# Down phase of a feed-forward layer: weight loads, block sums and residual tiles tied to other steps

## The chip, the cores and the metric

The program runs on one core of one Trainium2 chip, and nothing else runs beside it. The metric is the device time of one execution in microseconds. Lower is better. The time given for a kernel is the median of several executions; a profiled execution is one further execution, with its own time.

## What is computed

The kernel is one layer of a hybrid encoder on 2048 tokens of width 1024, in fp32: a mixing part (an FFT convolution and a bidirectional mLSTM), a cross-attention, and a feed-forward part with residual and a final normalization. Only the last part matters here:

```
h = h + square(relu(rms_norm(h, norm_ff_g) @ ff_w1)) @ ff_w2      # ff_w1: 1024 x 4096, ff_w2: 4096 x 1024
return rms_norm(h, final_norm_g)
```

## The kernel before

**Products in threes.** A matmul in full fp32 is made of three faster ones. A tile is split in a rounded high part and the remainder (`halves`, line 1620): ScalarE casts (L1622) and VectorE or GpSimd subtracts (L1623). `mm3` (line 352) then multiplies `ah` with `bh` (L354), `ah` with `bl` (L357) and `al` with `bh` (L358), in this order, where `ah` and `al` are the parts of a weight tile, `bh` and `bl` those of an activation tile. Both rings are short: four pairs of `ah`/`al`, six of `bh`/`bl`; the raw tiles `wr` that they are split from have six buffers (`raw`, line 1615).

**The feed-forward part** (`ffn`) works by a scheme of seven block products in place of eight. In the up phase the hidden activations and their combinations are written to DRAM (`hc`). The down phase multiplies them by combinations of the four quarters of each block of `ff_w2`. It goes over four blocks `o` of the hidden dimension. Each has seven products `i` in the order 1, 6, 7, 5, 3, 2, 4, each product has two token halves `tp`, and each of these four steps `k`. So there are 4 x 7 x 2 x 4 = 224 steps `s`, 56 for a block, eight for a product. A step is 12 matmuls on TensorE. Its result is gathered in four PSUM banks (named `mm` for the first token half and `hy` for the second) and, after the fourth step, added into the tile `acc[i, tp]` (line 1944).

**What a step writes beside its matmuls** (the loop over `down`, from line 1918):

- `fetch_b(s + 3)`: loads the activation tile of the step three further on (`wr<-hc`, L1617) and splits it (`bh`, `bl`).
- In the second token half `fetch_a(n + 1, k)`: makes the weight tile for the next product. For products 1, 6, 7 and 5 it comes from the twelve resident tiles `WD[k, 0..2]` (named `w` in the rows; a ring of 12 buffers), for 3, 2 and 4 it is loaded (`wr<-in_ff_w`, L1617), and for 3 `WD[k, 0]` is subtracted from it in place (L1750). The subtractions of `fetch_a` are VectorE's for the first six products and GpSimd's from the seventh on (product 4 of the first block).
- In product 2, first token half: `load_w(o + 1, k)` loads the three resident tiles of the next block for this `k` (L1757, SP's queue).
- In product 4, first token half: `sums_w(k)` forms two sums of them on GpSimd (L1760, L1761).
- From step 4 on, one `residual(i, tp, k)`: loads a tile of the residual stream into `acc` (`acc<-h`, L1867) and scales it on GpSimd (L1868); for i = 4 a second GpSimd operation follows (L1870). There are 32 of them, in the order i = 7, 4, 3, 2.

**What sets the order.** The code is written step by step, but a scheduler decides each engine's order by a simulated timeline, and puts an instruction as early as its inputs and buffers let it. A method `behind` (L362) holds an instruction back: it adds a dependency on the last matmul written so far, so that the scheduler places the instruction after that matmul. The dependency is of a class without synchronization: it shapes the order and leaves no semaphore wait on the chip. The loads are issued by SP, which works through its queue in order, as do the other engines.

Of the kernel before, what the change touches and what calls it, by code (L numbers as in the profile page):

```python
# [14 lines left out]
ALU = mybir.AluOpType  # L15
# [118 lines left out]
class Prog:  # L134
# [1592 lines left out]
    def ffn(self):  # L1727
        nc, tc, a = self.nc, self.tc, self.a
# [24 lines left out]
        def load_w(o, k):  # L1753
            w = self.blocks_of(2, 4 * o + k)
            for j, src in enumerate((w[0][0], w[1][0], w[1][1])):
                t = self.WD[k, j] = self.wtile()
                nc.sync.dma_start(out=t, in_=src)  # L1757

        def sums_w(k, op=nc.gpsimd.tensor_tensor):
            op(self.WD[k, 2], self.WD[k, 1], self.WD[k, 2], ALU.add)  # L1760
            op(self.WD[k, 1], self.WD[k, 0], self.WD[k, 1], ALU.subtract)  # L1761

        def fetch_b(s, eng=nc.vector):
            n, tp, k = down[s]
            o, i = prods[n]
            bq[s] = self.halves(self.raw(hc[tp, i - 1, 4 * o + k]), ("bh", "bl"), 6, eng)

        with tc.tile_pool(name="up", bufs=1) as U:
# [26 lines left out]
            for n, (tp, g, i) in enumerate(steps):  # L1795
# [11 lines left out]
                if n + 9 >= len(steps) and n + 5 < len(steps):  # L1807
                    load_w(0, n + 9 - len(steps))
                if n + 2 >= len(steps):
                    k = n + 2 - len(steps)  # L1810
# [20 lines left out]
                else:  # L1831
# [5 lines left out]
                    t = [self.stage() for _ in range(4)]  # L1837
                    op = nc.gpsimd.tensor_tensor
# [11 lines left out]
        with tc.tile_pool(name="down", bufs=1) as B:  # L1850
            acc, ms = {}, []
            on = [B.tile([128, D], F32, tag="on", name="on", bufs=2) for _ in range(2)]
            for tp in range(2):
                for h in range(2):
                    v = on[tp][:, 512 * h:512 * h + 512]
                    nc.sync.dma_start(out=v, in_=msd[2 * tp + h])
                    ms.append(v)
            for i in (1, 6, 7, 4, 5, 3, 2):
                for tp in range(2):
                    acc[i, tp] = B.tile([128, 4, 512], F32, tag="acc", name="acc", bufs=14)  # L1860
            gl = B.tile([128, D], F32, name="gl")
            nc.scalar.dma_start(out=gl, in_=a["final_norm_g"].unsqueeze(0).broadcast_to([128, D]))

            def residual(i, tp, k):
                n, h = {2: (0, 0), 7: (1, 1), 3: (1, 0), 4: (0, 1)}[i]
                v = acc[i, tp][:, k]
                nc.sync.dma_start(out=v, in_=h2[2 * tp + n, :, 4 * h + k])  # L1867
                nc.gpsimd.tensor_tensor(v, v, ms[2 * tp + n], ALU.mult)  # L1868
                if i == 4:
                    nc.gpsimd.tensor_tensor(v, v, acc[7, tp][:, k], ALU.subtract)  # L1870

            ss = B.tile([128, 4, 2, 4], F32, name="ss")

            def turn(c, h, src, dst, t, tag):
                pt = self.ps.tile([128, 512], F32, tag=tag, name=tag, bufs=4)
                for k in range(4):
                    nc.tensor.transpose(pt[:, 128 * k:128 * k + 128], src[:, k, 128 * t:128 * t + 128], self.ident)
                junk = B.tile([128, 512], F32, tag="junk", name="junk", bufs=1)
                nc.scalar.activation(junk, pt, AF.Square, accum_out=ss[:, c, h, t:t + 1])
                nc.vector.tensor_tensor(dst[:, t], pt, gl[:, 512 * h:512 * h + 512], ALU.mult)  # L1880

            def finish(c, dst):
                m = B.tile([128, 4], F32, tag="mo", name="mo", bufs=2)
                q = self.rbp[:, 4 * c:4 * c + 4]
                for h in range(2):
                    nc.vector.scalar_tensor_tensor(m, ss[:, c, h], 1.0 / D, m if h else q, ALU.mult, ALU.add)
                rv = self.rsqrt(B, m, "or")
                for t in range(4):
                    for h in range(2):
                        v = dst[h][:, t]  # L1890
                        if h and c % 2 == 0:
                            nc.vector.tensor_scalar(v, v, rv[:, t:t + 1], None, ALU.mult)
                        else:
                            nc.scalar.mul(v, v, rv[:, t:t + 1])
                        if t % 2:
                            r0 = 512 * c + 128 * (t - 1)
                            (nc.sync if h and c % 2 == 0 else nc.scalar).dma_start(
                                out=self.out[r0:r0 + 256, 512 * h:512 * h + 512].rearrange("(t p) c -> p t c", p=128),
                                in_=dst[h][:, t - 1:t + 1])

            def turned(c, tp, h, i, j, dst=None):
                def one(tag, t):
                    turn(c, h, acc[i, tp], acc[j, tp], t, tag)
                    if dst and t == 3:
                        finish(c, dst)
                return [lambda tag, t=t: one(tag, t) for t in range(4)]

            def add(i, j, tp, eng):
                for m in range(4):
                    eng.tensor_tensor(acc[i, tp][:, m], acc[i, tp][:, m], acc[j, tp][:, m], ALU.add)  # L1910

            early = [(i, tp, k) for i in (7, 4, 3, 2) for tp in range(2) for k in range(4)]
            outs = []
            V, G = nc.vector, nc.gpsimd
            for s, (n, tp, k) in enumerate(down):
                o, i = prods[n]
                if n == 0 and tp == 0:
                    sums_w(k, nc.vector.tensor_tensor)
                if s + 3 < len(down):
                    fetch_b(s + 3, G if s > 199 and k else V)  # L1920
                if o < 3 and tp == 0 and i == 2:
                    load_w(o + 1, k)
                if o < 3 and tp == 0 and i == 4:
                    sums_w(k)
                if early and s > 3:
                    residual(*early.pop(0))
                if k == 0:
                    bank = [self.hy() if tp else self.mm() for _ in range(4)]
                (ah, al), (bh, bl) = aq[n, k], bq.pop(s)
                for m in range(4):  # L1930
                    msl = slice(128 * m, 128 * m + 128)
                    self.mm3(bank[m], ah[:, msl], al[:, msl], bh, bl, k == 0, k == 3)
                if tp and n + 1 < len(prods):
                    fetch_a(n + 1, k)
                for _ in range(min(len(outs), 2 if len(outs) > 4 or n + 1 == len(prods) else 1)):
                    outs.pop(0)("mm" if tp else "hy")
                if k < 3:
                    continue
                for m in range(4):
                    v = acc[i, tp][:, m]  # L1940
                    if o == 0 and i in (1, 6, 5):
                        nc.scalar.copy(v, bank[m])
                    else:
                        d = nc.vector.tensor_tensor(v, bank[m], v, ALU.add)
                        if s + 1 == len(down):
                            tc.keep_in_program_order(d)
                if o < 3:
                    continue
                if i == 1:
                    add(2, 1, tp, G)  # L1950
                elif i == 6:
                    add(6, 1, tp, V)
                elif i == 7:
                    add(7, 6, tp, V)
                    add(3, 6, tp, G)
                elif i == 5:
                    add(3, 5, tp, V)
                    add(5, 7, tp, G)
                    add(4, 7, tp, G)
                    if tp:  # L1960
                        outs += turned(1, 0, 1, 5, 1)
                elif i == 3:
                    c = 2 * tp + 1
                    if not tp:
                        outs += turned(3, 1, 1, 5, 1)
                    outs += turned(c, tp, 0, 3, 6, (acc[6, tp], acc[1, tp]))
                elif i == 2:
                    outs += turned(2 * tp, tp, 0, 2, 7)
                elif i == 4:
                    outs += turned(2 * tp, tp, 1, 4, 5, (acc[7, tp], acc[5, tp]))  # L1970
            for x in outs:
                x("mm")
# [126 lines left out]
```

## Time and profile before

| what | value |
|---|---|
| time, median of 3 executions | 3133.62 us (3127.82 to 3135.12) |
| time of the profiled execution | 3131.11 us, its span 3129.0 us |
| mean granted clock of TensorE | 0.989 |
| busy share of the span: TensorE, its weight loads, VectorE, ScalarE, GpSimd | 97%, 76%, 63%, 48%, 37% |
| start of the down phase in the trace | about 2478 us |
| data moved | 607.07 MB, mean 194 GB/s |

How to read the rows: a row of a timeline has the start in us, the duration in us, the engine, the line, the operation, the tile written and the tiles read, and the count; in square brackets stands how long the engine stood idle before it and what ended that. Engines are PE (TensorE), PEld (its weight loads), DVE (VectorE), ACT (ScalarE), POOL (GpSimd) and SPq (SP's queue of DMA issues, with the time of issuing, not of the transfer). A row of a group has the count, then the busy time in us and the mean of one in ns, then the idle time before. A row of the windows has the stretch, its length, the busy time of PE, PEld, DVE, ACT and POOL, each with its number of instructions, then the granted clock of TensorE, the busy share of the DMA engines, and GB/s. A row of waits has who waited for whom, the us in total, how often, and the longest.

### The profile page before, as it was taken

Reading aid. Unit: us, or ns where it says so; the run is one execution under the profiler, and the core shown is the slowest. Engines: PE = TensorE matmul, PEld = TensorE weight load, DVE = VectorE, ACT = ScalarE, POOL = GpSimd, SP = SyncE. Lnnn points to the kernel's source line nnn. Section 1 sums busy time; section 2 is a strip of 40 time slices with the busy share of each in tenths; the row PEclk is TensorE's granted clock in tenths of the full one; section 3 lists DMA queues with packets and bytes.
Section 4 is the critical chain, followed back from the end, with each engine's and each line's share of the span. In section 5 each row is a group of like instructions: output and inputs, shape, how many; then the busy total and the mean of one; then the engine's idle time right before and its main releaser. Section 6 shows DMA issues by size and latency. Waiting matters only on the chain.

```text
span 3129.0 us, 42943 instructions
## 1 busy us (share of the span) xinstructions
PE 3029.1 (97%) x14257; PEld 2374.5 (76%) x14257; DVE 1964.8 (63%) x3448; ACT 1489.6 (48%) x2907; POOL 1146.9 (37%) x802
## 2 busy tenths in 40 slices
PE   8999999989999898999999999999999999999998
PEld 6655667766677666888887888888888878888876
DVE  7965466446646456777674656657545686555695
ACT  5443366533656225555544455556555533333335
POOL 0122012200113244324141337766456393434493
PEclk9999999999999999999999999999999999999999
DMA  6464767666878897455375657657644574434324
GB/s 212 153 210 163 235 203 220 194 215 216 241 206 249 261 316 245 145 190 186 127 268 186 217 166 243 207 178 231 205 152 153 179 234 142 152 123 152 122 91 172
DMA packets 444101, 607.07 MB, mean 194 GB/s; under 512 B 38494, under 2 KB 248542, under 8 KB 442856
## 3 DMA queue, kind: packets, MB, share of 16 engines
q1 hardware_dynamic: 405988, 546.54, 54.3%
q10 hardware_dynamic: 37892, 57.79, 5.3%
q8 instruction: 113, 1.85, 0.2%
q14 instruction: 108, 0.88, 0.1%
HBM read 401.79 MB, written 202.41 MB: 193 GB/s over the span
## 4 chain that ended last, share of the span: by engine, by line
PE 81%; DMA 7%; DVE 6%; ACT 3%; issue 2%; POOL 1%; SPq 0%; ACTq 0%; DVEq 0%; POOLq 0%
PE mm L354 17%; PE mm L358 17%; PE mm L357 17%; PE hy L358 5%; PE hy L354 5%; PE hy L357 5%; PE hy L177 3%; PE mm L912 1%; PE hy L943 1%; PE hy L985 1%; DMA xt<-in_x_t_dram 1%; DVE bl L1623 1%; PE mm L674 1%; DMA a<-hy 1%; PE mm L703 1%
## 5 line engine op out<-in xcount | busy, mean ns | idle before, releaser
L1623 DVE TENSOR_TENSOR bl<-wr,bh 128x512 fp32r<-128x512 f32 x213 | 239.8, 1132 | 132.5 <-ACT bh L1622 132.3
L1622 ACT CAST ah<-w 128x512 fp32r<-128x512 f32 x284 | 176.9, 624 | 302.5 <-PE hy L357 155.8
L365 DVE TENSOR_TENSOR wl<-wn,wh 128x512 fp32r<-128x512 f32 (+1 forms) x300 | 217.6, 772 | 102.7 <-ACT wh L365 102.4
L354 PE MATMUL mm<-xh,wh 128*128 128x512 f32 x640 | 267.7, 419 | 12.2 <-ACT wh L365 9.1
L990 POOL TENSOR_TENSOR b<-b,a 128x512 f32<-128x512 f32 x64 | 87.0, 1362 | 510.1 <-ACT b L988 320.0
L357 PE MATMUL mm<-xl,wh 128*128 128x512 f32 x640 | 255.8, 400 | 0.7 <-DVE xl L365 0.6
L1622 ACT CAST bh<-wr 128x512 fp32r<-128x512 f32 x232 | 143.8, 622 | 234.6 <-PE mm L358 176.2
L358 PE MATMUL mm<-xh,wl 128*128 128x512 f32 x640 | 255.0, 399 | 0.0
L1623 DVE TENSOR_TENSOR al<-w,ah 128x512 fp32r<-128x512 f32 x236 | 217.6, 922 | 54.9 <-ACT ah L1622 54.9
L358 PE MATMUL mm<-bh,al 128*128 128x512 f32 x576 | 224.1, 392 | 6.8 <-DVE al L1623 4.3
L354 PE MATMUL mm<-bh,ah 128*128 128x512 f32 x576 | 225.7, 392 | 0.5 <-DVE acc L1780 0.4
L357 PE MATMUL mm<-bl,ah 128*128 128x512 f32 x576 | 224.9, 390 | 0.0
L365 ACT CAST wh<-wn 128x512 fp32r<-128x512 f32 (+1 forms) x300 | 167.4, 620 | 110.4 <-PE mm L358 52.1
L357 PE MATMUL mm<-act,wh 128*128 128x512 f32 x512 | 200.5, 393 | 0.8 <-DVE act L365 0.8
L354 PE MATMUL mm<-act,wh 128*128 128x512 f32 x512 | 198.4, 393 | 1.1 <-ACT wh L365 0.9
L358 PE MATMUL mm<-act,wl 128*128 128x512 f32 x512 | 199.1, 392 | 0.3 <-DVE wl L365 0.3
L354 PE MATMUL hy<-bh,ah 128*128 128x512 f32 x448 | 175.2, 391 | 0.0
L357 PE MATMUL hy<-bl,ah 128*128 128x512 f32 x448 | 174.6, 390 | 0.0
L358 PE MATMUL hy<-bh,al 128*128 128x512 f32 x448 | 174.4, 390 | 0.0
L354 PEld LDWEIGHTS mm<-xh,wh 128*128 128x128 f32 x640 | 121.4, 190 | 67.6 <-issue 19.0
L354 PE MATMUL mm<-wh,xh 128*128 128x256 f32 (+1 forms) x512 | 155.7, 305 | 13.0 <-ACT xh L365 10.6
L336 POOL TENSOR_TENSOR b<-b 128x512 f32<-128x512 f32 x32 | 58.3, 1822 | 277.8 <-DVE b L333 137.2
(369 smaller groups left out, 8285.4 us busy)
## 6 DMA issues: line engine op xcount, KB each, us to landing
wr<-hc SPq DMA_DIRECT2D x224, 256.0 KB
w<-in_ff_w_dram SPq DMA_DIRECT2D x172, 256.0 KB
hc<-wn SPq DMA_DIRECT2D x128, 256.0 KB
wn<-in_w_in_dram SPq DMA_DIRECT2D x100, 256.0 KB
hc<-q SPq DMA_DIRECT2D x96, 256.0 KB
fs<-a SPq DMA_DIRECT2D x32, 512.0 KB
a<-fs SPq DMA_DIRECT2D x64, 256.0 KB
a<-zs SPq DMA_DIRECT2D x64, 256.0 KB
```

Source lines behind the costliest of these rows:

```text
L177: b = self.nc.tensor.matmul(*products[-1], start=True, stop=True)
L336: nc.gpsimd.tensor_tensor(e[1], f, b, ALU.subtract)
L354: first = mm(ps, lh, rh, start=start, stop=False)
L357: mm(ps, lh, rl, start=False, stop=False)
L358: self.last = mm(ps, ll, rh, start=False, stop=stop)
L365: both = (self.nc.scalar.copy(hi, src), self.nc.vector.tensor_tensor(lo, src, hi.bitcast(F32), ALU.subtract))
L674: mul(p[:, m], w[:, k, ms], mt[k // 4][:, k % 4], start=k == 0, stop=k == 7)
L703: mul(p, t[:, m, ms], o_[:, m, ds], start=m == 0, stop=m == 1)
L912: nc.tensor.matmul(pp, dm[:, m], t[:, m], start=True, stop=True)
L990: nc.gpsimd.tensor_tensor(xt, xt, hi[:, m], ALU.mult)
L1622: self.nc.scalar.copy(hi, src)
L1623: eng.tensor_tensor(lo, src, hi.bitcast(F32), ALU.subtract)
```

## The change

Three things are edited. The weight loads of the blocks 1 to 3 are held behind the last matmul written before them, which bars the scheduler from placing them ahead of the step in product 2 that they are written in. The eight sums of each next block on GpSimd are held the same way, in product 4. And from step 20 on a residual tile is written in two of three steps, not in each.

```
-                nc.sync.dma_start(out=t, in_=src)
-
-        def sums_w(k, op=nc.gpsimd.tensor_tensor):
-            op(self.WD[k, 2], self.WD[k, 1], self.WD[k, 2], ALU.add)
-            op(self.WD[k, 1], self.WD[k, 0], self.WD[k, 1], ALU.subtract)
+                d = nc.sync.dma_start(out=t, in_=src)
+                if o:
+                    self.behind(d)
+
+        def sums_w(k, op=nc.gpsimd.tensor_tensor, late=False):
+            a = op(self.WD[k, 2], self.WD[k, 1], self.WD[k, 2], ALU.add)
+            b = op(self.WD[k, 1], self.WD[k, 0], self.WD[k, 1], ALU.subtract)
+            if late:
+                self.behind(a)
+                self.behind(b)
...
                 if o < 3 and tp == 0 and i == 4:
-                    sums_w(k)
-                if early and s > 3:
+                    sums_w(k, late=True)
+                if early and (3 < s < 20 or s > 19 and s % 3):
                     residual(*early.pop(0))
```

Line numbers behind the edit grow by two to five: L1760, L1761, L1868 and L1944 of before are L1762, L1763, L1873 and L1949 of the change, L1867 and L1870 are L1872 and L1875. The numbers behind tile names are counted through the program and differ a little between the two.

**First place: the weight tiles of product 3 in the first block.** On SP, before: `wr_23074` and `wr_23101` are the third and fourth of the four weight tiles that product 3 loads, the `wr` from `hc` are activation tiles, `w` are resident tiles of the next block, `acc_22315` and `acc_22316` are residual tiles of i = 2.

```order
L1617 DMA wr_23074<-in_ff_w2_dram 128x512
L1617 DMA wr_23081<-hc_16691 128x512
L1757 DMA w_23388<-in_ff_w2_dram 128x512
L1867 DMA acc_22315<-h2_10617 128x512 x4
L1617 DMA wr_23101<-in_ff_w2_dram 128x512
L1617 DMA wr_23112<-hc_16691 128x512
L1757 DMA w_23390<-in_ff_w2_dram 128x512
```

The same stretch of SP in the change, from the same third weight tile (here `wr_23066`) on; the fourth is `wr_23093`.

```order
L1617 DMA wr_23066<-in_ff_w2_dram 128x512
L1617 DMA wr_23073<-hc_16691 128x512
L1617 DMA wr_23093<-in_ff_w2_dram 128x512
L1617 DMA wr_23104<-hc_16691 128x512
L1617 DMA wr_23128<-hc_16691 128x512
L1617 DMA wr_23146<-hc_16691 128x512
L1617 DMA wr_23166<-hc_16691 128x512
L1617 DMA wr_23190<-hc_16691 128x512
L1872 DMA acc_22315<-h2_10617 128x512 x3
L1617 DMA wr_23212<-in_ff_w2_dram 128x512
```

The loads of `w` have left this stretch, and the residual tiles of i = 2 stand behind five activation tiles that follow the fourth weight tile. VectorE at the same place, before (`al_23024` is the first weight tile of product 3, ready for TensorE):

```order
L1750 TENSOR_TENSOR wr_23074<-wr_23074,w_22103 128x512
L1623 TENSOR_TENSOR bl_23030<-wr_23027,bh_23029 128x512
L1623 TENSOR_TENSOR bl_23057<-wr_23054,bh_23056 128x512
L1750 TENSOR_TENSOR wr_23101<-wr_23101,w_22127 128x512
L1623 TENSOR_TENSOR al_23024<-wr_23020,ah_23023 128x512
```

and in the change:

```order
L1750 TENSOR_TENSOR wr_23066<-wr_23066,w_22103 128x512
L1623 TENSOR_TENSOR bl_23024<-wr_23021,bh_23023 128x512
L1750 TENSOR_TENSOR wr_23093<-wr_23093,w_22127 128x512
L1623 TENSOR_TENSOR bl_23051<-wr_23048,bh_23050 128x512
L1623 TENSOR_TENSOR al_23018<-wr_23014,ah_23017 128x512
```

The fourth L1750 has moved ahead of one `bl`; the first `al` still stands behind it. Nothing else moves on VectorE, and the orders of TensorE and ScalarE are the same as before.

**Second place: GpSimd in the first block.** Before, from the residual tiles of i = 3, second half, on; the sums of the next block are L1760 and L1761:

```order
L1868 TENSOR_TENSOR acc_22314<-acc_22314,on_22298 128x512 x4
L1760 TENSOR_TENSOR w_23314<-w_23312,w_23314 128x512
L1760 TENSOR_TENSOR w_23342<-w_23340,w_23342 128x512
L1761 TENSOR_TENSOR w_23312<-w_23310,w_23312 128x512
L1761 TENSOR_TENSOR w_23340<-w_23338,w_23340 128x512
L1760 TENSOR_TENSOR w_23366<-w_23364,w_23366 128x512
L1761 TENSOR_TENSOR w_23364<-w_23362,w_23364 128x512
L1868 TENSOR_TENSOR acc_22315<-acc_22315,on_22297 128x512 x4
L1760 TENSOR_TENSOR w_23390<-w_23388,w_23390 128x512
L1761 TENSOR_TENSOR w_23388<-w_23386,w_23388 128x512
L1868 TENSOR_TENSOR acc_22316<-acc_22316,on_22298 128x512 x4
L1623 TENSOR_TENSOR al_23433<-wr_23430,ah_23432 128x512
```

and in the change, from the same residual tiles on; the `al` are the four weight tiles of product 4:

```order
L1873 TENSOR_TENSOR acc_22314<-acc_22314,on_22298 128x512 x4
L1873 TENSOR_TENSOR acc_22315<-acc_22315,on_22297 128x512 x4
L1873 TENSOR_TENSOR acc_22316<-acc_22316,on_22298 128x512 x4
L1623 TENSOR_TENSOR al_23433<-wr_23430,ah_23432 128x512
L1623 TENSOR_TENSOR al_23457<-wr_23454,ah_23456 128x512
L1762 TENSOR_TENSOR w_23308<-w_23306,w_23308 128x512
L1763 TENSOR_TENSOR w_23306<-w_23304,w_23306 128x512
L1623 TENSOR_TENSOR al_23481<-wr_23478,ah_23480 128x512
L1762 TENSOR_TENSOR w_23338<-w_23336,w_23338 128x512
L1623 TENSOR_TENSOR al_23505<-wr_23502,ah_23504 128x512
L1762 TENSOR_TENSOR w_23364<-w_23362,w_23364 128x512
L1763 TENSOR_TENSOR w_23336<-w_23334,w_23336 128x512
```

The eight sums have moved from among the residual tiles to behind the second `al` of product 4; three of them stand ahead of the last two `al`. In the other two blocks the sums move to the same place.

**Third place: the loads of the next block on SP, in the second block.** Before (names without numbers here, since only the kinds matter), from the loads in product 7 on:

```order
L1757 DMA w<-in_ff_w_dram 128x512 x2
L1617 DMA wr<-hc 128x512
L1757 DMA w<-in_ff_w_dram 128x512
L1617 DMA wr<-hc 128x512 x5
L1617 DMA wr<-in_ff_w_dram 128x512
L1757 DMA w<-in_ff_w_dram 128x512
L1617 DMA wr<-hc 128x512
L1757 DMA w<-in_ff_w_dram 128x512 x3
L1617 DMA wr<-in_ff_w_dram 128x512
```

and in the change, where all twelve stand beside product 2 (the `wr` from `in_ff_w` are weight tiles of product 4):

```order
L1617 DMA wr<-hc 128x512 x3
L1757 DMA w<-in_ff_w_dram 128x512 x3
L1617 DMA wr<-hc 128x512 x2
L1757 DMA w<-in_ff_w_dram 128x512 x3
L1617 DMA wr<-in_ff_w_dram 128x512
L1617 DMA wr<-hc 128x512
L1757 DMA w<-in_ff_w_dram 128x512 x3
L1617 DMA wr<-in_ff_w_dram 128x512
L1617 DMA wr<-hc 128x512
L1757 DMA w<-in_ff_w_dram 128x512 x3
```

The loads that were strewn over some twenty `wr` loads from product 7 to product 3 now stand in four triples.

## The prediction

> **What bounds the kernel.** I read the page's busy table first, then the down phase in slices of 100 us, then TensorE's own waits there.
>
> ```profile
> span 3129.0 us, 42943 instructions
> PE 3029.1 (97%) x14257; PEld 2374.5 (76%) x14257; DVE 1964.8 (63%) x3448; ACT 1489.6 (48%) x2907; POOL 1146.9 (37%) x802
> ```
>
> ```profile
> 2400.00:2500.00 100.00, 99.51 (x437) 81.62 (x437) 61.97 (x82) 49.85 (x86) 44.08 (x30) 1.00 0.50 167
> 2500.00:2600.00 100.00, 95.75 (x416) 78.83 (x416) 79.47 (x75) 41.15 (x73) 77.25 (x48) 0.98 0.71 238
> 2600.00:2700.00 100.00, 100.00 (x443) 82.84 (x442) 57.26 (x73) 32.98 (x56) 33.55 (x25) 1.00 0.38 120
> 2900.00:3000.00 100.00, 100.00 (x443) 82.84 (x442) 69.97 (x81) 31.94 (x54) 55.82 (x37) 1.00 0.35 108
> ```
>
> ```profile
> PE mm L358 <- DVE al L1623: 4.3, 1, 4.3
> PE mm L354 <- DVE acc L1780: 0.4, 1, 0.4
> ```
>
> The change acts only between the start of the down phase, near 2478, and the loads of its last block. From 2600 to 3000 TensorE is busy in every microsecond at the full granted clock (1.00), so nothing is to be won there. The waits of TensorE from 2478 to 3000 are two, and one of them is 4.3 us long. All that the change can win is this one wait and what hangs on it. Here it is, on TensorE's own timeline:
>
> ```profile
> 2564.87 0.39 PE L354 MATMUL mm<-bh,ah 128*128 128x512 f32 x1
> 2565.10 0.39 PE L357 MATMUL mm<-bl,ah 128*128 128x512 f32 x1
> 2569.74 0.79 PE L358 MATMUL mm<-bh,al 128*128 128x512 f32 x1 [4.25 <-DVE al L1623]
> 2570.33 0.63 PE L354 MATMUL mm<-bh,ah 128*128 128x512 f32 x1
> ...
> 2572.88 0.39 PE L354 MATMUL mm<-bh,ah 128*128 128x512 f32 x1
> ```
>
> Matmuls start 0.227 us apart (2564.87 to 2565.10), so a step of 12 takes 2.72 us. The third matmul of step 32 (product i = 3, first k) was due at 2565.33 and came at 2569.74, 4.41 us late, because it needs `al` from VectorE. Behind it seven starts lie 0.43 to 0.59 us apart: at 0.227 us they would have brought TensorE from 2565.33 to 2566.92, and the trace has 2572.88. So the stall costs **5.96 us**: 4.41 of waiting and 1.55 of slow matmuls. Who made `al` late?
>
> ```profile
> 2553.92 3.47 DVE L1623 TENSOR_TENSOR bl<-wr,bh 128x512 fp32r<-128x512 f32 x2
> 2558.39 0.70 DVE L1750 TENSOR_TENSOR wr<-wr,w 128x512 f32<-128x512 f32 x1 [0.99 <-DMA wr<-in_ff_w_dram]
> 2559.01 3.47 DVE L1623 TENSOR_TENSOR bl<-wr,bh 128x512 fp32r<-128x512 f32 x2
> 2567.19 0.82 DVE L1750 TENSOR_TENSOR wr<-wr,w 128x512 f32<-128x512 f32 x1 [4.70 <-DMA wr<-in_ff_w_dram]
> 2567.93 1.75 DVE L1623 TENSOR_TENSOR al<-wr,ah 128x512 fp32r<-128x512 f32 x1
> 2575.28 0.68 DVE L1623 TENSOR_TENSOR bl<-wr,bh 128x512 fp32r<-128x512 f32 x1
> ```
>
> ```profile
> 2555.73 0.33 SPq L1617 DMA_DIRECT2D wr<-in_ff_w_dram  x1
> 2557.42 0.33 SPq L1617 DMA_DIRECT2D wr<-hc  x1
> 2559.12 0.33 SPq L1757 DMA_DIRECT2D w<-in_ff_w_dram  x1
> 2559.50 1.85 SPq L1867 DMA_DIRECT2D acc<-h  x4
> 2561.45 0.38 SPq L1617 DMA_DIRECT2D wr<-in_ff_w_dram  x1
> 2562.51 0.32 SPq L1617 DMA_DIRECT2D wr<-hc  x1
> ```
>
> ```profile
> 2548.77 6.38 POOL L1868 TENSOR_TENSOR acc<-acc,on 128x512 f32<-128x512 f32 x4
> 2555.11 3.43 POOL L1760 TENSOR_TENSOR w<-w 128x512 f32<-128x512 f32 x2
> 2564.96 5.85 POOL L1868 TENSOR_TENSOR acc<-acc,on 128x512 f32<-128x512 f32 x4
> 2578.10 5.60 POOL L1868 TENSOR_TENSOR acc<-acc,on 128x512 f32<-128x512 f32 x4 [3.90 <-DMA acc<-h]
> ```
>
> VectorE works in order. Ahead of the `al` stands the fourth subtraction of L1750, which waits 4.70 us for its weight tile. That load could be issued when a `wr` buffer came free (a `bl` that ended at 2560.74, half of the 3.47 us from 2559.01), but SP was still writing out four residual loads, and issued it at 2561.45. It landed at 2567.1, 5.7 us later, behind those four and a `w`; the same load issued at 2555.73 had landed by 2558.3, 2.6 us later. Two things made the row late: the extra loads on SP, and GpSimd. While GpSimd works, a `bl` takes 1.74 us (3.47 for two); alone it takes 0.68.
>
> **The change, part by part.** *Weight loads* (12 a block, 36 in all): the same loads, moved on SP. In the first block they leave the stretch ahead of product i = 3, and so do the four residual loads at 2559.50, which now stand behind five more `hc` loads. The dependency on the last matmul binds the scheduler alone: SP and GpSimd get no wait on TensorE from it, so nothing new is queued behind such a wait. *Block sums* (8 a block, 24 in all): moved on GpSimd from 2555 to product i = 4. *Residual tiles*: 32 as before; the first 24 stay where they were in GpSimd's order but for one exchange, the last eight come later. Their loads stand behind `hc` loads that follow VectorE's buffers one by one, to about 2568.5 by the walk below, and 2.6 us to land makes 2571. No instruction is added, and the order of TensorE and ScalarE is unchanged; on VectorE one L1750 stands one place earlier.
>
> Walk VectorE through the new order. GpSimd runs its 24 residual tiles to 2555.15 as before (2548.77 + 6.38) and then has nothing to do until the last eight land. So from there VectorE's 1.74 becomes 0.68. The two `bl` that started at 2553.92 end near 2555.4 and 2556.1. The third weight tile is issued at 2555.4 and lands at 2558.0 (2.6 us); L1750 to 2558.7; `bl` to 2559.4, which frees the buffer for the fourth tile; with nothing ahead of it on SP it lands at 2562.0; L1750 to 2562.7, the `bl` that now stands behind it to 2563.4, `al` to **2564.1**. It is due at 2565.33, so 1.2 us are to spare. The next `al` has a `bl` ahead whose row was loaded at 2556.1: done at 2565.5, due at 2568.05. So the stall goes, with a thin margin. What is late next is this same chain: two loads of 2.6 us one behind the other. The wait that is left is bounded by 0 and 4.41; I take 0.4, nearer to 0, since only a load slowed by 1.2 us brings it back.
>
> [...]
>
> **Costs.** The last eight residual tiles (1.6 each, 12.8 us) now run near 2571 to 2584 on GpSimd beside products i = 3 and 2. A step then needs a `bl`, an `al` (1.74 each) and 0.68 for a drain (L1944 below, four in four steps): 4.2 us against 2.72, for about five steps, 7.4 us in all. The cover is the three steps (8.2 us) that an `al` has between the end of the matmuls that free its buffer and its own use, and VectorE is by then ahead of TensorE and waiting for buffers. Price 0, or at the most a wait like the one removed, 5.96; I take 0. Then the three places where the moved loads and sums land:
>
> ```profile
> L1761 POOL TENSOR_TENSOR w<-w 128x512 f32<-128x512 f32 x12 | 19.1, 1599 | 0.5
> L1760 POOL TENSOR_TENSOR w<-w 128x512 f32<-128x512 f32 x12 | 18.3, 1525 | 6.5 <-PE hy L358 3.4 <-DMA w<-in_ff_w_dram 2.9 <-POOL wr L1750 0.2
> L1623 POOL TENSOR_TENSOR al<-wr,ah 128x512 fp32r<-128x512 f32 x40 | 54.3, 1361 | 96.3 <-ACT ah L1622 96.3
> L1622 ACT CAST ah<-wr 128x512 fp32r<-128x512 f32 x48 | 29.8, 622 | 51.8 <-PE hy L357 32.3 <-POOL al L1623 18.9 <-POOL bl L1623 0.6
> L1944 DVE TENSOR_TENSOR acc<-hy,acc 128x512 f32<-128x512 f32 x100 | 64.3, 680 | 16.7 <-PE hy L358 16.7
> ```
>
> ```profile
> ACT bh L1622 <- PE mm L358: 146.0, 73, 2.1
> ACT bh L1622 <- DMA wr<-hc: 1.4, 2, 1.1
> ```
>
> Eight sums are 4 x 1.60 + 4 x 1.53 = 12.5 us of GpSimd. Three of them (4.7 us) stand ahead of the last two `al` of product 4; an `al` of 1.36 behind its cast of 0.62 has 8.2 us, and 4.7 + 1.36 + 0.62 = 6.7, so it fits. The other five (7.8 us) run while GpSimd waits for buffers anyway. VectorE beside a busy GpSimd needs 1.74 + 0.68 = 2.4 of 2.72 us a step, since from product 4 on the `al` are GpSimd's. Price 0; a longer queue would cost a wait as above. The loads (256.0 KB each): three `w`, one `hc` and one weight tile a step for four steps, 5 x 262,144 bytes in 2.72 us, or 482 GB/s. The trace's fullest slice shows less:
>
> ```profile
> w<-in_ff_w_dram SPq DMA_DIRECT2D x36, 256.0 KB
> ```
>
> ```profile
> 2500.00:2510.00 10.00, 10.00 (x45) 8.27 (x45) 8.11 (x8) 6.20 (x13) 7.61 (x5) 1.00 1.04 397
> ```
>
> At 397 GB/s four steps leave 0.92 MB over, 2.3 us of lateness. ScalarE's `bh` casts wait for TensorE to free a buffer (146.0 us from 2600 to 3000) and hardly for loads (1.4 us), so a late load first eats this room. Price 0; from the other side three stalls of 5.96, 17.9 us. [...]
>
> **Sum.** 0.4 - 5.96 = -5.5 us. The profiled execution took 3131.1 us (span 3129.0 and 2.1 around it), so 3125.6; the median of the three runs, 3133.6, lies 2.5 above it, which gives 3128.1. I forecast **3127**, between the two.
>
> **Rivals.** *The wait stays.* The fourth tile's load still waits for a `bl` and holds VectorE up. If it takes 5.7 us and not 2.6, `al` comes at 2567.2, 1.9 us late: 3131.1 - 5.96 + 1.9 = 3127.0, with the median's offset 3129.5. If the third tile is as slow, `al` is 5.0 us late and the whole stall is back: 3131.1 to 3133.6. For it speaks the thin margin; against it, that the loads which slowed the row are gone from around it. *The loads queue up* (the slower side): the four triples of `w` are in front of `hc` and weight rows on SP, and a row that lands more than 6.2 us late (8.2 less a cast and an `al`) stops ScalarE's in-order casts and then TensorE, as at 2565. It decides from a lateness of 6.2 us; the 2.3 reckoned stay below. If it does, in all three blocks: 3131.1 - 5.5 + 17.9 = 3143.5, with the median's offset up to 3146. *Nothing changes*: if 2565 had another cause than the loads, the time stays at 3131 to 3134. I count it with the wait that stays. *More than the stall is won*: the span after 3000 would have to shrink, but no engine's order differs there.
>
> **Chances.** Stall gone 0.75; wait stays or nothing changes 0.15; loads queue up 0.06; more won 0.04. About 0.3% (9.4 us) is what a measurement of this kernel can tell from no change; the runs before span 7.3 us. The forecast lies inside it. Faster by over 0.3% takes the last case, and the first with medians that err by 4 us: 0.09. Slower by over 0.3%: 0.06. Within: 0.85. The range goes from the fastest run less the whole stall (3127.8 - 5.96 = 3121.9) to the case in which nothing changes with the slowest run, rounded up: 3136.
>
> **What would show it.** Right: no wait of TensorE for `al` near 2565, its slice 2560 to 2580 full at clock 1.00, GpSimd idle from 2555 to about 2571, `bl` at 0.68 in that stretch, the fourth L1750 waiting some 2.6 us instead of 4.70, and 2600 to 3000 still full. Wrong: a wait for `al` in steps 32 to 35 of the first block, or TensorE idle at the change of product 2 to 4 in any block, with ScalarE's `bh` casts waiting for `hc` loads there.

## The result, and the profile after

| | before | after |
|---|---|---|
| median of 22 executions each, us | 3133.66 (3127.10 to 3141.83) | 3127.52 (3122.69 to 3134.73) |
| ratio after to before, 95% interval | | 0.9981 (0.9975 to 0.9987) |
| span of the profiled execution, us | 3129.0 | 3125.4 |
| start of step 32 on TensorE in that span, us | 2564.87 | 2567.33 |
| from there to the end of the span, us | 564.1 | 558.1 |

The change makes the kernel 0.19% faster, 6.1 us by the medians; the forecast was 3127. The two spans differ by 3.6 us only, since in the profile of after the down phase begins 2.46 us later, after parts of the program that the change does not touch. From step 32 to the end the difference is 6.0 us. That stretch is the sharper measure, and I use it below for single profiles.

TensorE's waits between 2478 and 3000 in the profile of after are down to one:

```profile
PE mm L354 <- DVE acc L1785: 0.3, 1, 0.3
```

The same stretches as before, in the windows (columns as before: length, busy PE, PEld, DVE, ACT, POOL, clock, DMA share, GB/s):

```profile
2500.00:2600.00 100.00, 100.00 (x443) 82.79 (x442) 81.17 (x82) 43.93 (x79) 65.19 (x40) 1.00 0.69 236
2600.00:2700.00 100.00, 100.00 (x443) 82.81 (x442) 60.70 (x76) 33.56 (x57) 46.22 (x33) 1.00 0.40 121
2900.00:3000.00 100.00, 100.00 (x443) 82.81 (x442) 75.29 (x83) 31.95 (x55) 71.63 (x47) 1.00 0.39 122
2560.00:2580.00 20.00, 20.00 (x90) 16.56 (x89) 13.29 (x18) 7.44 (x14) 6.70 (x4) 1.00 0.69 224
```

From 2500 to 2600 TensorE was busy for 95.75 us and is now for 100.00. GpSimd's work moves out of that stretch (77.25 to 65.19 us) and into later ones (33.55 to 46.22 and 55.82 to 71.63 in the two rows below it), where TensorE stays full. Here is step 32 on TensorE, with its third matmul (L358) right behind the second:

```profile
2567.33 0.39 PE L354 MATMUL mm<-bh,ah 128*128 128x512 f32 x1
2567.56 0.39 PE L357 MATMUL mm<-bl,ah 128*128 128x512 f32 x1
2567.79 0.39 PE L358 MATMUL mm<-bh,al 128*128 128x512 f32 x1
```

And the chain that feeds it, first VectorE, then SP, then GpSimd:

```profile
2556.24 2.38 DVE L1623 TENSOR_TENSOR bl<-wr,bh 128x512 fp32r<-128x512 f32 x2
2560.70 0.69 DVE L1750 TENSOR_TENSOR wr<-wr,w 128x512 f32<-128x512 f32 x1 [2.08 <-DMA wr<-in_ff_w_dram]
2561.31 0.68 DVE L1623 TENSOR_TENSOR bl<-wr,bh 128x512 fp32r<-128x512 f32 x1
2564.64 0.69 DVE L1750 TENSOR_TENSOR wr<-wr,w 128x512 f32<-128x512 f32 x1 [2.65 <-DMA wr<-in_ff_w_dram]
2565.25 0.68 DVE L1623 TENSOR_TENSOR bl<-wr,bh 128x512 fp32r<-128x512 f32 x1
2565.86 0.69 DVE L1623 TENSOR_TENSOR al<-wr,ah 128x512 fp32r<-128x512 f32 x1
```

```profile
2562.02 0.33 SPq L1617 DMA_DIRECT2D wr<-in_ff_w_dram  x1
2565.97 4.34 SPq L1617 DMA_DIRECT2D wr<-hc  x5
2570.36 1.37 SPq L1872 DMA_DIRECT2D acc<-h  x3
```

```profile
2551.07 6.40 POOL L1873 TENSOR_TENSOR acc<-acc,on 128x512 f32<-128x512 f32 x4
2573.30 12.85 POOL L1873 TENSOR_TENSOR acc<-acc,on 128x512 f32<-128x512 f32 x8 [15.83 <-DMA acc<-h]
```

The fourth weight tile is issued at 2562.02, right as the `bl` from 2561.31 ends, and is used 2.62 us later, where it was 5.74 (2561.45 to 2567.19) before. VectorE's operations take 0.68, while GpSimd stands idle for 15.83 us. `al` ends at 2566.55 and is due at 2567.79, so 1.24 us are to spare.

### The profile page after: what moved, and what is told of

Same layout as the page of the kernel before. It is cut to its first block, busy times and chain, and to the rows that moved or that the text cites. A ratio compares the mean times of both kernels' runs of the same rounds, so it can differ in the third digit from the quotient of the medians.

```text
span 3125.4 us, 42916 instructions
## 1 busy us (share of the span) xinstructions
PE 3031.2 (97%) x14257; PEld 2377.4 (76%) x14257; DVE 1960.3 (63%) x3448; ACT 1487.1 (48%) x2907; POOL 1146.5 (37%) x802
## 4 chain that ended last, share of the span: by engine, by line
PE 84%; DMA 6%; DVE 4%; ACT 2%; issue 2%; POOL 1%; SPq 0%; ACTq 0%; DVEq 0%; POOLq 0%
PE mm L354 17%; PE mm L358 17%; PE mm L357 17%; PE hy L358 6%; PE hy L354 6%; PE hy L357 6%; PE hy L177 3%; PE mm L912 2%; PE hy L943 2%; PE hy L985 1%; DMA a<-hy 1%; PE hy L1279 1%; PE mm L674 1%; PE mm L703 1%; PE hy L1281 1%
## 5 line engine op out<-in xcount | busy, mean ns | idle before, releaser
L358 PE MATMUL mm<-xh,wl 128*128 128x512 f32 x640 | 254.8, 399 | 0.0
L358 PE MATMUL mm<-bh,al 128*128 128x512 f32 x576 | 224.0, 391 | 2.6 <-POOL al L1623 2.6
L358 PE MATMUL mm<-act,wl 128*128 128x512 f32 x512 | 199.1, 392 | 0.0
L358 PE MATMUL hy<-bh,al 128*128 128x512 f32 x448 | 174.4, 390 | 0.0
```

The lines of the kernel that those rows point to most:

```text
L358: self.last = mm(ps, ll, rh, start=False, stop=stop)
```

## The experiments

The question was which of the three edits took the stall away, and by which of the two causes that the prediction named: loads ahead of the fourth tile on SP, or GpSimd beside VectorE. In the table, "tile" is the time from the fourth weight tile's issue on SP to the start of the L1750 that uses it, "late" is how far the third matmul of step 32 started behind its due time (the start of the step's first matmul and two spacings of 0.227), and "rest" is from step 32's start to the end of the span, all from the profile of the run. The ratio is to the kernel before on the same chip, with its 95% interval; the kernel with two ahead and two behind was executed once only. All these kernels were built from the kernel after, so their rows have its line numbers; each edit below is shown by its effect.

| kernel | residual loads right ahead of the tile | tile, us | late, us | rest, us | ratio |
|---|---|---|---|---|---|
| before | 4 | 5.74 | 4.41 | 564.1 | |
| sums held only | 4 | 5.18 | 4.40 | 565.3 | 0.9997 (0.9987 to 1.0008) |
| loads and sums held | 4 | 4.50 | 2.23 | 562.6 | 0.9983 (0.9974 to 0.9992) |
| two ahead, two behind | 2 | 3.11 | 0 | 558.8 | |
| residuals thinned only | 0 | 2.75 | 0.81 | 560.9 | 0.9979 (0.9971 to 0.9988) |
| four residuals deferred only | 0 | 2.67 | 0.86 | 560.5 | 0.9984 (0.9975 to 0.9993) |
| sums held, residuals thinned | 0 | 2.96 | 0 | 558.1 | 0.9968 (0.9955 to 0.9980) |
| the same again | 0 | 2.97 | 0 | 558.1 | 0.9988 (0.9979 to 0.9997) |
| loads held, residuals thinned | 0 | 2.64 | 0 | 558.1 | 0.9978 (0.9970 to 0.9987) |
| all three (after, again) | 0 | 2.69 | 0 | 558.2 | 0.9979 (0.9969 to 0.9990) |

The ratios are coarser than their intervals say: the same kernel twice (sums held, residuals thinned) gave 0.9968 and 0.9988, with intervals that barely meet. And "loads and sums held" is some 5 us faster than before by its ratio but 1.5 us by its rest; its profiled execution was the slowest of its eleven. The argument therefore goes by "tile" and "late", each from one profiled execution of its kernel, and how much a wait varies between executions was not measured. The rests of the kernels that have no wait at step 32 agree within 0.1 us, but for the one with two ahead, which has a longer wait near the end (see the last section).

### Block sums alone

Edit, from the kernel before:

```
-                    sums_w(k)
+                    sums_w(k, late=True)
```

> Only the block sums are held to product 4; weight loads and residual tiles stand as before the change. Three theories of the 4.41 us wait at step 32. T (both causes): the fourth weight tile is late because of the loads ahead of it on SP and because VectorE runs at 1.74 us an operation beside GpSimd. G: GpSimd's work beside VectorE alone. L: the loads on SP alone. Here GpSimd is free from its 24th residual tile on (2555 in the time of before), but four residual loads and the w loads still stand ahead of the fourth tile. T: bl at 0.68, fourth tile issued about 1 us earlier (2559.7 to 2560.5), still 5 to 6 us to land; a wait of about 2.2 us (0.5 to 3.4) is left; 3130.5 us. G: no wait, 3127.5 us. L: the wait stays at 3.5 to 4.4 us, 3133 us.

Measured: 3134.03 us, ratio 0.9997 (0.9987 to 1.0008), `al` 4.40 us late. G falls and L's numbers hold; T's 2.2 us of wait was wrong too. VectorE's last three operations ahead of the fourth tile took 0.69 us or less each, and that gained nothing. Behind it GpSimd's residual tiles slowed L1750 to 1.03 and `al` to 1.75, which is 1.4 us of the 4.40. VectorE, then SP:

```profile
2560.43 0.69 DVE L1750 TENSOR_TENSOR wr<-wr,w 128x512 f32<-128x512 f32 x1 [2.65 <-DMA wr<-in_ff_w_dram]
2561.04 1.29 DVE L1623 TENSOR_TENSOR bl<-wr,bh 128x512 fp32r<-128x512 f32 x2
2568.66 1.03 DVE L1750 TENSOR_TENSOR wr<-wr,w 128x512 f32<-128x512 f32 x1 [6.33 <-DMA wr<-in_ff_w_dram]
2569.62 1.75 DVE L1623 TENSOR_TENSOR al<-wr,ah 128x512 fp32r<-128x512 f32 x1
```

```profile
2561.15 0.33 SPq L1757 DMA_DIRECT2D w<-in_ff_w_dram  x1
2561.53 1.85 SPq L1872 DMA_DIRECT2D acc<-h  x4
2563.48 0.39 SPq L1617 DMA_DIRECT2D wr<-in_ff_w_dram  x1
```

The `bl` at 2561.04 is two in one row, so the buffer for the fourth tile came free near 2561.7. But SP issued the tile at 2563.48: the `w` load ahead of it came at 2561.15, right as the third L1750, which reads the old `w`, had ended, and the four residual loads stood behind that `w`. The faster VectorE had only more time to wait, 6.33 us where it was 4.70. While the tile was under way, the DMA engines were nearly full, as the window of this run shows (share 0.92, 294 GB/s), against 0.29 in the profile of after in the same place:

```profile
2562.00:2568.00 6.00, 5.20 (x23) 3.96 (x22) 0.33 (x1) 0.21 (x1) 2.60 (x3) 1.00 0.92 294
```

```profile
2562.00:2565.00 3.00, 3.00 (x15) 2.49 (x14) 0.35 (x1) 0.69 (x2) 0.00 (x0) 1.00 0.29 87
```

The `w`, four residual tiles and the weight tile are 6 x 262,144 bytes, 5.3 us at 294 GB/s; the tile was used 5.2 us after its issue. The tiles with no residual load ahead were used 2.62 to 2.97 us after their issue; 5.18 is far above that and fits the loads queued ahead.

### Residual tiles alone

Edit, from the kernel before:

```
-                if early and s > 3:
+                if early and (3 < s < 20 or s > 19 and s % 3):
```

> Only the later residual tiles are thinned to two steps in three; weight loads and sums stand as before the change. The four residual loads are gone from ahead of the fourth weight tile, but GpSimd adds block sums until about 2567 (8 of 1.56 us from 2555). T: the tile lands 2.6 to 4 us after its issue at 2560.8, but the subtraction, the bl and the al behind it take 1.7 us each, so al is still about 3.2 us late (2.5 to 4.3); 3131 to 3133 us. L: no wait or under 1 us; 3127.5 us. G: the wait stays at 4 us or more, 3133.5 us; T and G differ here only in the load's time to land.

Measured: 3129.79 us, 0.9979 (0.9971 to 0.9988), 0.81 us late. The wait is L's number, and T's 3.2 us fell for the second time; the median lies between L's 3127.5 and T's 3131 to 3133, on a chip on which the kernel before took 3135.94 us. The tile's 2.75 us are those of after, with block sums still beside VectorE:

```profile
2566.58 0.33 SPq L1617 DMA_DIRECT2D wr<-in_ff_w_dram  x1
```

```profile
2569.33 1.53 DVE L1750 TENSOR_TENSOR wr<-wr,w 128x512 f32<-128x512 f32 x1 [2.78 <-DMA wr<-in_ff_w_dram]
2570.79 0.68 DVE L1623 TENSOR_TENSOR bl<-wr,bh 128x512 fp32r<-128x512 f32 x1
2571.39 0.68 DVE L1623 TENSOR_TENSOR al<-wr,ah 128x512 fp32r<-128x512 f32 x1
```

GpSimd's sums slowed this L1750 (1.53 for 0.69) and the `bl` before it (1.77 for 0.68), but then GpSimd ran into a wait of its own (3.68 us for an `al`), and `bl` and `al` ran at 0.68. T had charged the slow rate for all three.

### Sums held and residuals thinned, loads as before

Edit, from the kernel after:

```
-                if o:
-                    self.behind(d)
```

> Sums held and residual tiles thinned, weight loads as before the change: every engine but SP has the order of the changed kernel, and only the 12 w loads a block lie earlier on SP, among the loads of products 7, 5 and 3. T: the tile lands 2.6 to 4 us after its issue, al is done up to 1.2 us before it is due or 0.3 us after; no wait over 0.3 us, 3127.5 us. That the w loads are what slows the row (L, in the form of bandwidth): a wait of 1.5 us or more stays, 3129.5 us or more. The moved weight loads would then be worth nothing by T, and the change could do without them.

Measured: 3126.46 us (0.9968, 0.9955 to 0.9980), no wait, rest 558.1. The fourth tile was used 2.96 us after its issue, with the `w` loads still around it. L's other form, in which the `w` loads slow the row by bandwidth, falls: it asked for a wait of 1.5 us or more. So with the other two edits in place, the hold on the weight loads is worth nothing at step 32.

### Loads and sums held, residual tiles as before

Edit, from the kernel after:

```
-                if early and (3 < s < 20 or s > 19 and s % 3):
+                if early and s > 3:
```

> Weight loads and sums held, residual tiles as before the change: four residual loads stand right ahead of the fourth weight tile on SP, and GpSimd works on them as soon as they land. T: those four loads are issued some 3 us earlier than before, since no w load is ahead of them; the tile lands at about 2562 to 2563.5, then GpSimd's residual tiles slow the subtraction and al to 1.7 us each; a wait of about 0.9 us (0 to 2), 3128.5 us. L: with the four loads still ahead the tile takes over 5 us; wait 1.5 to 3 us with VectorE at 0.68 to 1.7, 3130 to 3131 us. G: no block sums, but residual tiles in the same place; wait 2 us or more, 3130 us.

Measured: 3130.48 us (0.9983, 0.9974 to 0.9992), 2.23 us late; L expected 1.5 to 3, T about 0.9. SP, then VectorE:

```profile
2562.98 1.85 SPq L1872 DMA_DIRECT2D acc<-h  x4
2566.27 0.33 SPq L1617 DMA_DIRECT2D wr<-in_ff_w_dram  x1
```

```profile
2570.77 1.35 DVE L1750 TENSOR_TENSOR wr<-wr,w 128x512 f32<-128x512 f32 x1 [3.93 <-DMA wr<-in_ff_w_dram]
2572.05 1.75 DVE L1623 TENSOR_TENSOR al<-wr,ah 128x512 fp32r<-128x512 f32 x1
```

The four residual loads were issued at 2562.98 and the tile at 2566.27, and GpSimd began on the first of them only at 2567.80. Against the run with the sums held only, this kernel differs by the hold on the weight loads, and its wait is 2.17 us shorter. No `w` that waits for L1750 stands in front any more, so SP issued the residual loads 3.3 us ahead of the tile, and the tile 1.8 us earlier against the time that `al` is due; the tile itself took 0.68 us less. This run also shows what a wait of half the size of before's does to TensorE (the four matmuls left out start 0.23 to 0.34 us apart):

```profile
2571.39 0.39 PE L357 MATMUL mm<-bl,ah 128*128 128x512 f32 x1
2573.85 0.50 PE L358 MATMUL mm<-bh,al 128*128 128x512 f32 x1 [2.07 <-DVE al L1623]
...
2575.14 0.63 PE L357 MATMUL mm<-bl,ah 128*128 128x512 f32 x1
2575.57 0.63 PE L358 MATMUL mm<-bh,al 128*128 128x512 f32 x1
2575.99 0.63 PE L354 MATMUL mm<-bh,ah 128*128 128x512 f32 x1
```

TensorE resumed at full spacing and 1.3 us later fell to 0.43 for eight matmuls; in all 3.96 us were lost for a wait of 2.23.

### The four residual loads alone

Edit, from the kernel before:

```
-                if early and s > 3:
+                if early and s > 3 and not 27 < s < 32:
```

> The kernel before with one edit: no residual tile is started in steps 28 to 31, so that the four residual loads ahead of the fourth weight tile stand behind five more hc loads; weight loads and block sums as before. After the first four runs the theory is Q: those four loads are the cause, by the 1.85 us that SP needs to write them and by their transfer in front of the tile's; the sums beside VectorE set only the last us. Q: the tile lands 2.6 to 3 us after its issue, a wait of 0.5 to 1.5 us is left (VectorE still at 1.7 us beside the sums), 3128 to 3130 us, a ratio to before near 0.998. If instead the thinning of all later tiles is what helped, the wait stays above 3 us and the time within 1 us of before.

Measured: 3129.25 us (0.9984, 0.9975 to 0.9993), 0.86 us late, tile 2.67 us. Holding eight residual tiles back by four steps, in one block, takes 3.55 of the 4.41 us away. SP, then VectorE:

```profile
2559.88 0.33 SPq L1617 DMA_DIRECT2D wr<-in_ff_w_dram  x1
```

```profile
2562.55 1.62 DVE L1750 TENSOR_TENSOR wr<-wr,w 128x512 f32<-128x512 f32 x1 [2.69 <-DMA wr<-in_ff_w_dram]
```

The tile takes 3.07 us less (5.74 to 2.67) and is issued 0.80 us earlier against the time that `al` is due; VectorE's operations from L1750 to `al` take 0.32 us more. What is left of the wait goes with VectorE's slow L1750 (1.62 us), as with the thinned residuals.

### Weight loads held and residuals thinned, sums as before

Edit, from the kernel after:

```
-                    sums_w(k, late=True)
+                    sums_w(k)
```

> Weight loads held and residual tiles thinned as in the changed kernel, but the block sums not held: TensorE, VectorE, ScalarE and SP have the order of the changed kernel, and on GpSimd all eight sums of a block stand ahead of the four al of product 4. The prediction's price of 0 for the sums: they start with the w rows at about 2590, end by 2604 (12.5 us, or the last row at 2600 and 3 us), the first al is done by 2606 and due at 2611; no wait in any of the three blocks, 3127.5 us as the changed kernel. If GpSimd's queue has no such room, TensorE waits for al at product 4 in three blocks, 2 to 6 us each, 3134 us or more.

Measured: 3129.26 us (0.9978, 0.9970 to 0.9987), no wait of TensorE from 2478 to 3000, rest 558.1. Against the thinned residuals alone, this kernel differs by the hold on the weight loads, and the wait of 0.81 us is gone: since the held loads bring the `w` late, the sums could not start early either. The eight sums ran from 2595.23 to 2608.5, four us later than expected, and the first `al` of product 4 behind them ended near 2610, with TensorE due at 2612.6. So even the whole of the sums ahead of the `al` fits.

### All twelve loads of a block at once

Edit, from the kernel after:

```
-                    load_w(o + 1, k)
+                    [load_w(o + 1, j) for j in range(0 if k else 4)]
```

> The changed kernel with the 12 w loads of a block issued together in the first step of product 2, not three in each of four steps: 3.15 MB, 7.9 us at 397 GB/s, ahead of the next hc row, which then lands about 4 us later than in the changed kernel. The prediction's slower rival decides from a lateness of 6.2 us: by it 7.9 is 1.7 us too many in each of three blocks, 3132 to 3137 us, with TensorE waiting near 2598 and at the same place in the next blocks. If the room is larger (six bh buffers let ScalarE cast five steps, 13.6 us, ahead), no wait, 3127.5 us.

Measured: 3127.79 us (0.9977, 0.9967 to 0.9986), no wait. ScalarE stood still for 9.66 us for the `hc` row behind the twelve loads:

```profile
2600.54 1.31 ACT L1622 CAST bh<-wr 128x512 fp32r<-128x512 f32 x2 [9.66 <-DMA wr<-hc]
2602.48 0.62 ACT L1622 CAST bh<-wr 128x512 fp32r<-128x512 f32 x1 [0.62 <-DMA wr<-hc]
2603.77 0.62 ACT L1622 CAST bh<-wr 128x512 fp32r<-128x512 f32 x1 [0.67 <-DVE acc L1949]
2606.12 0.62 ACT L1622 CAST bh<-wr 128x512 fp32r<-128x512 f32 x1 [1.21 <-PE hy L358]
```

The cast at 2606.12 waited for TensorE to free one of six buffers, by ending the step before the one that it began at 2605.89 (step 46). It therefore is for step 51, and the five casts in these rows are those of steps 47, 48, 49, 50 and 51. Step 47 began at 2608.61, 8.1 us after its cast. Its buffer had come free with the end of step 41 at 2595.0, so the cast was 5.5 us late and could have been some 7 us later still. The room is thus five steps (13.6 us) less a cast and a `bl`, about 12 us, where the prediction had 6.2. That is read from these times: the 5.5 us of lateness in this run are below both bounds, so that TensorE did not wait would fit either. In this burst the DMA engines moved this:

```profile
2595.00:2600.00 5.00, 5.00 (x24) 4.13 (x23) 0.00 (x0) 0.00 (x0) 0.00 (x0) 1.00 1.06 406
```

### The margin

Edit, from the kernel after, for the first weight tile of product 3 in the first block only (three subtractions with the same result):

```
-        eng.tensor_tensor(lo, src, hi.bitcast(F32), ALU.subtract)
+        [eng.tensor_tensor(lo, src, hi.bitcast(F32), ALU.subtract) for _ in range(more)]
```

> The changed kernel with the subtraction that makes the al of step 32 done three times over (the same result): two more VectorE instructions of 0.6 us, behind a bl, so al is done at 2568.4 in the time of the changed kernel's trace, against 2567.79 when it is due. If the margin is the 1.24 us read there, TensorE waits 0.6 us and no matmul behind it is slow; if the next wait is hidden elsewhere, none; if any wait here draws slow matmuls, about 2 us are lost.

Measured: 3130.34 us (one execution), 1.22 us late and no slow matmul behind. In this profile the first of the three subtractions ended at 2567.91 with 2568.68 due, a margin of 0.77; the other two and the `bl` between are 1.8 us, so 1.0 was to be expected from there. Over the profiles of kernels without a wait the margin is 0.4 (2.96 us tile) to 1.24 us. It is as thin as predicted, and it moves between executions.

### Two loads ahead, two behind

Edit, from the kernel after:

```
-                if early and (3 < s < 20 or s > 19 and s % 3):
+                if early and s > 3 and not 29 < s < 32:
```

> The changed kernel, but two residual loads stand right ahead of the fourth weight tile on SP and two right behind it (the kernel with four ahead needed 4.50 us from issue to use of the tile, the changed kernel with none 2.62). Q, each load ahead takes its share of the transfer: 2.62 + 2 x 0.47 to 0.66 = 3.6 to 3.9 us, a wait of about 0.8 us (0 to 1.5) with GpSimd's residual tiles beside VectorE. If all loads near the tile share the transfer with it, those behind it too: 4.5 us and a wait of about 2 us. If only the time to write the loads counts: 2.6 us and no wait.

Measured: 3129.94 us (one execution), no wait, tile 3.11 us. That all loads near the tile share the transfer falls. Two ahead and two behind together cost 0.5 us against after (2.62), so those behind cost little or nothing, and two ahead at most half of what Q expected: GpSimd began on the first of them at 2564.38, just as the tile was issued (2564.16), so one was through by then. With four ahead and held loads GpSimd began only 1.5 us after the tile's issue. Four ahead cost 1.9 to 3.1 us more than none (the longest two with a `w` among them), and they bring the stall; two do not, and three were not tried.

### After once more, and without the hold on the loads

The first run is the kernel after as it is, the second that without the hold on the loads, by the edit shown for it.

> The changed kernel itself, as the yardstick for the next run on one chip. Ratio to before near 0.998, no wait of TensorE from 2500 to 3000.

> Sums held and residual tiles thinned, the weight loads left where they were (its first measurement: 0.9968 of before, from 5 runs). If moving the weight loads is worth nothing, this is equal to the changed kernel within the interval of some 0.1%; if the loads at product 2 cost something that TensorE's waits do not show, it is 0.1% (3 us) faster.

Measured on one chip: after 3127.66 us (0.9979, 0.9969 to 0.9990), without the hold on the loads 3129.07 us (0.9988, 0.9979 to 0.9997). The intervals overlap, and both rests are the same (558.2 and 558.1); that it could be 0.1% faster without the hold did not show. The 0.9968 of its first measurement did not come again. No version beat the kernel after: from step 32 to 3000 TensorE has nothing left to gain.

## Why the prediction was right

**What bounds.** Right. The one wait was all there was to win: 564.1 to 558.1 us, 6.0, against 5.96 reckoned from the spacing of the matmuls. The forecast's 0.4 of leftover wait was 0. The prediction took 0.3% as the least that a measurement can tell; with 22 executions each, 0.19% stands clear of no change (0.9975 to 0.9987).

**The walk of VectorE.** Right to 0.1 us. Predicted: fourth tile 2.6 us to land, waiting time of L1750 about 2.6, `bl` at 0.68, margin of `al` 1.2. Measured: 2.62, 2.65, 0.68, 1.24. GpSimd's idle stretch and the last eight residual tiles (12.85 us from 2573.30, that is 2570.84 in the time of before) came as walked, at price 0.

**The cause.** Half right. "The extra loads on SP, and GpSimd" do not count alike. The four residual loads are the cause of most of it: deferring only them leaves 0.86 of 4.41 us, while holding the sums alone leaves 4.40. With the residual loads gone, GpSimd's sums are worth the last 0.8 us, and either hold takes them away: that on the sums, or that on the `w` loads, by which the sums come late too. The `w` loads, which the prediction named beside the residual ones, have no price of their own. With the residual loads still there (and the sums held), the hold on the `w` takes the wait from 4.40 to 2.23; with both other edits in place it takes nothing, as two measurements without it show (tile at 2.96 and 2.97 us, no wait). So the thinned residuals and one of the two holds do the work at step 32. The hold on the weight loads alone was not run. After the result alone, the three would have looked alike.

**The prices of 0.** Right in value. The bound behind the slower rival was mis-sized, by the term "three steps (8.2 us)" less a cast and an `al`, 6.2 us. The six `bh` buffers let ScalarE run five steps ahead, which makes about 12 us, and even all twelve loads at once made no wait. The rival that the loads queue up was thus further away than the prediction reckoned. In that burst the DMA engines moved 406 GB/s from 2595 to 2600, where the prediction had reckoned with 397, and TensorE did not wait.

**The clock.** The rival in which the wait stays counts a wait of 1.9 us with no slow matmuls behind it. No run has a wait of that length at step 32: waits up to 1.22 us drew none there, and the run with 2.23 us drew eight and lost 3.96 us in all, 1.7 of it after the wait. By proportion to the row of before (1.55 behind 4.41) those 1.7 would have been 0.8. No term of the sum hung on this, since no wait was left.

**The offset to the median.** The profile-based sum of 3125.6 and the median-based 3128.1 bracket the 3127.5 measured. That 3127 came within 0.5 us is luck in part: the interval of the ratio alone is about 1.9 us to either side.

## What to carry to other kernels

Where one engine waits for a load, first read what stands ahead of that load on its issuing queue, and how full the DMA engines are while it is under way: here four 256-KB loads that could come 8 us later at no cost stood in front of one that was needed at once, and most of a 6-us stall came from that. Then ask what else on that queue waits in front of such loads: here one that waited for an engine made them later still, and without it the wait was 2.17 us shorter. Speeding up an engine that waits for a late load only lengthened its wait here (VectorE's, from 4.70 to 6.33 us), so undo the queue first. And take room in a pipeline from the number of buffers, not from how many steps ahead the code writes the load (about 12 us here, where the count of three steps gave 6.2).

## What the runs showed of the hardware that was not expected

The clock after a wait is not a matter of its length alone. Waits up to 1.22 us drew no slow matmuls (three profiles), 2.23 us drew eight and 4.4 us seven and ten. But one and the same wait, near the end of the down phase, where the change does nothing, went both ways. Before, then after:

```profile
3031.32 0.50 PE L358 MATMUL mm<-bh,al 128*128 128x512 f32 x1 [2.35 <-POOL al L1623]
3031.66 0.39 PE L354 MATMUL mm<-bh,ah 128*128 128x512 f32 x1
3031.89 0.40 PE L357 MATMUL mm<-bl,ah 128*128 128x512 f32 x1
```

```profile
3027.80 0.74 PE L358 MATMUL mm<-bh,al 128*128 128x512 f32 x1 [2.35 <-POOL al L1623]
3028.34 0.63 PE L354 MATMUL mm<-bh,ah 128*128 128x512 f32 x1
3028.77 0.63 PE L357 MATMUL mm<-bl,ah 128*128 128x512 f32 x1
```

Both waited 2.35 us for the same `al` of GpSimd. Before went on at 0.23 between starts with a granted clock of 1.00 (3031.3 to 3034.0), after at 0.43 for seven matmuls with 0.51 (3027.8 to 3031.0). At step 32 of before the granted clock was still 1.00 at 2569.25, 3.8 us into the wait, and 0.50 from 2569.50 to 2572.50. Five of the timelines have the later wait at 2.35 us, and slow matmuls follow it in three of them. Why the same wait goes both ways stays open.

In three kernels (residuals thinned only, four deferred only, two ahead) this later wait is about 3.0 us instead of 2.35. With the loss at step 32 (about 1.0, 1.0 and 0) this makes up 1.7, 1.6 and 0.6 of the 2.8, 2.4 and 0.7 us that their rests have over that of after. The remainder lies mostly behind this wait and was not traced, and what lengthens the wait was not tried.
